# A hybrid decoder step on one core: weight splits in half-size pieces through two rooms, gate scratch in a tile of its own, and later stores of the compression weights

## The chip, the cores and the metric

The kernel runs on one core of a Trainium2 chip. The time is the device time of one execution in microseconds (us); the kernel before was run three times. All sizes are fixed: 1024 prompt tokens, 8 sample tokens with 2048 cached tokens each, model width 1024.

## What is computed

One layer of a decoder with two parallel head groups, cut to what matters here:

```python
h = rms_norm(x, norm_g); proj = h @ w_in
b_gate, c_gate, conv_in, z_conv, q, kv, gate_logits, z_attn = split(proj)
# group 1: short convolution over the tokens
conv = b_gate * short_conv(c_gate * conv_in) * silu(z_conv)
# group 2: sparse attention, three branches per query block of 128 tokens
kv_cmp = compress_blocks(kv[cmp], cmp_pe, cmp_w)        # 32 tokens -> 1 row
o = g0 * attend(q, kv_cmp) + g1 * attend(q, top blocks) + g2 * attend(q, last 512 tokens)
attn = o * silu(z_attn)
y = x + concat(conv, attn) @ w_out                       # 1024 x 1024
```

The prompt goes through this with its own keys and values, the 8 samples with gathered cache rows. Outputs are y, the new key/value rows and the conv state.

## The kernel before, in words

All large products are in float32 split into two parts: a high part, which ScalarE (ACT) makes as a rounding copy (`copy`, line 75), and a low part, the difference, which VectorE (DVE) or GpSimd (POOL) subtracts (`sub`, line 79). A product is three matmuls of such parts (lines 227 to 229 for the channel products, `chan_mm`).

The program has two long stages that run as merged streams (`merge`, line 30: generators give costs, and the stream that is least far along is recorded next) and then a last one. The tile framework orders the instructions of each engine from this and from the tiles' readers and writers; each engine runs its list in order, and so does the queue that SyncE (SP) feeds.

1. `phase0` (line 534): norm, key/value and query projections. In its second loop over 9 token tiles, `cw_fetch` and `cw_split` bring in the compression weights `cw` and split them; for t = 5 to 8 line 595 stores a quarter of them (`cw_d`, a DRAM scratch), and after the loop line 607 multiplies with them. From here to 236 us the rest of the projections follow.
2. The attention of the prompt, `attn_stream` (line 762): 32 units, 8 query blocks `qi` of 128 tokens x 2 groups x 2 head pairs. A unit does, for branch 1 (selected and compressed, tiles `P1a` and `P0`) and branch 2 (window, tile `P2`): `scores` (matmuls `s`, line 804, then `softmax`, the row maximum and mask on DVE, line 792, and the exponent on ACT, line 794), `scale` (reciprocal on DVE, 844; gate and denominator on POOL, 849 and 853), then transposes (`pt`, 878), their split into `ph` and `pl`, and the products `o` (888). `double` (770) and `prep` (776, then `q`) make the next unit's queries; `finish` (903) multiplies into `mixA`. Beside it runs `conv_stream`: channel products `mm` from weights `wraw` that SP loads (line 173) and ACT and POOL split into `wh` and `wl`; `conv_use` (line 707) consumes them. A z product ends in `silu2` (line 699): tanh on ACT from the bank (line 700, `mixC<-mm`), then a product on DVE (line 701).
3. Samples, output projection: `prefetch` loads `wo_d` and `cw_d` back through the POOL queue, and so on to the end at 937.5 us.

Two side jobs ride on the first units of stage 2, and they are what the change touches.

- `w_split` (line 908): the first 512 columns of `w_out`, 8 row chunks. Even unit 2k loads chunk k (256 KB, line 914) into the low half of a tile `P1b`; odd unit 2k+1 splits it (ACT copy of 512 columns, POOL subtraction of 512 columns) and stores both halves to `wo_d[k]` (512 KB, line 918). The tile has one room: the load of chunk k+1 overwrites what the store of chunk k reads. From query block 4 on, the attention itself uses the tile `P1b`.
- `z_attn` (line 703): the silu of z for the attention's own gate, one piece of 128 tokens (4 channels x 128 = 512 columns) for each query block. Its tanh goes into the scratch tile `acc` (one room), which `conv_use` (line 719) also uses for the convolution.

```python
if ui % 2 == 0:
    wsp = at.tile([128, 2, 512], F32R, name="P1b")
    SP.dma_start(f(wsp[:, 1]), w_out[:, ui // 2, 0:512])
else:
    copy(ACT, wsp[:, 0], f(wsp[:, 1]))
    sub(POOL, wsp[:, 1], f(wsp[:, 1]), f(wsp[:, 0]))
    SP.dma_start(wo_d[ui // 2], f(wsp))
```

Of the kernel before, what the change touches and what calls it, by code (L numbers as in the profile page):

```python
# [60 lines left out]
def hymba_step_kernel(ctx, tc, io):  # L61
# [8 lines left out]
    def f(ap):  # L70
        return ap.bitcast(F32)
# [6 lines left out]
    def sub(eng, out, a, b):  # L78
        return eng.tensor_tensor(out, a, b, OP.subtract)  # L79
# [455 lines left out]
    def phase0():  # L535
        nonlocal qkv
        x_load(0)
        SP.dma_start(gbc, bcast_rows(io["norm_g"], D))
        SP.dma_start(idt, io["c_ident"])
        c0 = wl0(COL_KV, 256)  # L540
        c0[1](0)
        c0[1](1)
        x_load(1)
        c0[1](2, xsp)
        c0[1](3, xsp)
        x_load(2)
        SP.dma_start(rope0, io["c_rope"])
        turns = [x_norm(0)]
        turns.pop(0)()
        tab0 = rope_tables(io["k_gain"][0, 0], 0, 1.0)  # L550
        for i in range(4):
            c0[2](i, *E0)
        x_load(3)
        turns.append(x_norm(1))
        turns.pop(0)()
        c1 = wl0(COL_KV + 256, 256)
        for t in range(NT):
            if t + 4 < NT:
                x_load(t + 4)
            if t + 2 < NT:  # L560
                turns.append(x_norm(t + 2))
            o = tok_mm(t, c0[0], 256)
            if turns:
                turns.pop(0)()
            posted(1)
            rows, _ = kv_rows(wk, o, t, 0, *tab0)
            if t < 8:
                posts.append((lambda kd=twice(wk, rows, 4), t=t: cmp_transposes(kd, t), 1))
            if t == 7:
                tab1 = rope_tables(io["k_gain"][0, 1], 1, 1.0)  # L570
            if t in (1, 2):
                for i in (2 * t - 2, 2 * t - 1):
                    c1[2](i)
            if t < 2:
                for i in (2 * t, 2 * t + 1):
                    c1[1](i)
            yield 3900
        posted(9)
        xss.close()
        cw = xcp2.enter_context(pool("cw")).tile([128, 16, 2, 128], F32R, name="cw")  # L580
        c2 = wl0(COL_KV + 512, 280)
        for t in range(NT):
            kv_tile(t, c1[0], 256, 1, tab1)
            if t == SM:
                small_things()
            if t == 0:
                c2[1](0)
                c2[1](1)
            if t in (2, 4):
                c2[2](t // 2 - 1)  # L590
                c2[1](t // 2 + 1)
            if 0 < t < 5:
                cw_split()
            if t > 4:
                SP.dma_start(cw_d[t - 5], f(cw[:, t * 4 - 20:t * 4 - 16]))
            if t < 4:
                cw_split = cw_fetch(wk, cw, t)
            yield 3400

        posted(9)  # L600

        kc = wk.tile([128, 2, 2, 33], F32, name="kc")
        for j in range(2):
            o = bank("cc")
            for rho in range(16):
                for X in (XH, XL):
                    PE.matmul(o[:, :66], cw[:, rho, j], X[:, 2 * j:2 * j + 2, rho::16],
                              start=rho == 0 and X is XH, stop=rho == 15 and X is XL)
            ov = o[:, :66].rearrange("p (g c) -> p g c", g=2)
            copy(ACT, kc[0:64, j], ov[64:128])  # L610
            copy(ACT, kc[64:128, j], ov[0:64])
            DVE.tensor_tensor(kc[:, j], ov, kc[:, j], OP.add)
            copy(DVE, pew[:, j:j + 1], kc[:, j, 0, 32:33])
            DVE.tensor_scalar(kc[:, j, :, :32], kc[:, j, :, :32], pew[:, j:j + 1], None, op0=OP.add)
        copy(ACT, kpc, kc[:, 0, :, :32])
        sub(DVE, kpc[64:128], kc[64:128, 0, :, :32], f(kpc[64:128]))
        p = bank("tp")
        for g in range(2):
            PE.transpose(p[:32, g * 64:g * 64 + 64], kc[0:64, 1, g, :32], ident[:64, :64])
        pv = p[:32, :128].rearrange("p (g d) -> p g d", g=2)  # L620
        copy(ACT, vpc[:32, :, 0:64], pv)
        sub(DVE, vpc[:32, :, 64:128], pv, f(vpc[:32, :, 0:64]))
        yield 8000
        xcp2.close()
        xcs.close()

        qkv = left.enter_context(pool("qkv"))
        K[2] = qkv.tile([128, 2, SEQ], F32R, name="k2")
        V[2] = qkv.tile([128, 8, 2, 128], F32R, name="v2")
        qt.extend(qkv.tile([128, 512], F32, name=f"q{t}") for t in range(8))  # L630

        c2[2](2)
        c2[2](3)
        tab2 = rope_tables(io["k_gain"][0, 2], 0, 1.0)
        nxt = wl0(COL_Q, 256)
        for t in range(NT):
            kv_tile(t, c2[0], 280, 2, tab2)
            if t == 0:
                nxt[1](0)
                nxt[1](1)  # L640
            if t in (2, 4):
                nxt[2](t // 2 - 1)
                nxt[1](t // 2 + 1)
            yield 3600
        posted(9)
        tabq = rope_tables(io["q_gain"][0], 1, 0.125)
        for which in range(2):
            nxt[2](2)
            nxt[2](3)
            w = nxt[0]  # L650
            nxt = wl0(COL_Q + 256, 256)
            for t in (8, *range(8)):
                q_tile(t, w, which, tabq)
                if which == 0:
                    if t == 0:
                        nxt[1](0)
                        nxt[1](1)
                    if t in (2, 4):
                        nxt[2](t // 2 - 1)
                        nxt[1](t // 2 + 1)  # L660
                yield 2700
# [30 lines left out]
    cvs = ExitStack()  # L692
    cv = cvs.enter_context(pool("conv", "right"))
    cu = cv.tile([128, 2 + NTOK], F32, name="cu")
    uo = cv.tile([128, 4, 16], F32, name="uo")
    POOL.memset(cu[:, 0:2], 0.0)

# [3 lines left out]
        DVE.scalar_tensor_tensor(m, t, 1.0, z, op0=OP.add, op1=OP.mult)  # L701

    def z_attn(a, n):
        t = cv.tile([128, 512], F32, name="acc")[:, :4 * n].rearrange("p (a c) -> p a c", a=4)
        silu2(mixA[:, :, a:a + n], mixA[:, :, a:a + n], t)

    def conv_use(kind, i, c, o, s):
# [7 lines left out]
        else:  # L715
            DVE.tensor_tensor(u, o, u, OP.mult)
            n = CH if c < 2 else SEQ - 2 * CH
            w, b = cvw[:, i, :], cvw[:, i, 3:4]
            acc = cv.tile([128, 512], F32, name="acc")
            a, lo = acc[:, :n], c * CH  # L720
            ACT.activation(a, cu[:, lo:lo + n], AF.Copy, scale=w[:, 0:1])
            for r in (1, 2):
# [12 lines left out]
    def conv_stream():  # L735
        yield from chan
        p = bank("mm")
        for i in range(4):
            PE.transpose(p[:10, i * 128:(i + 1) * 128], uo[:, i, :10], ident)
        ur = cv.tile([128, 512], F32, name="acc")[:10]  # L740
        copy(ACT, ur, p[:10])
        SP.dma_start(io["p_conv"].rearrange("l b r c -> (l b r) c"), ur[0:2])
        SP.dma_start(io["s_conv"].rearrange("l b r c -> (l b) r c")[:, 1, :], ur[2:10])
        yield 400

    at = left.enter_context(pool("attn"))
# [15 lines left out]
    def attn_stream():  # L762
# [141 lines left out]
            if g == 1 and hp == 1:  # L904
                done[qi] = True

        wsp = None

        def w_split(ui):

            nonlocal wsp
            if ui % 2 == 0:
                wsp = at.tile([128, 2, 512], F32R, name="P1b")
                SP.dma_start(f(wsp[:, 1]), w_out[:, ui // 2, 0:512])
            else:
                copy(ACT, wsp[:, 0], f(wsp[:, 1]))
                sub(POOL, wsp[:, 1], f(wsp[:, 1]), f(wsp[:, 0]))
                SP.dma_start(wo_d[ui // 2], f(wsp))

        qq = prep(double(units[0]))  # L920
        masks()
        pend = []
        for ui, u in enumerate(units):
            o = [None]
            share = PACE[u[0]]
            if ui % 4 == 2 and u[0] < 7:
                z_attn(u[0] * 128 + 128, 128)
            elif ui == 3:
                z_attn(SEQ, 8)
            a = at.tile([128, 1024], F32, name="P1a")  # L930
            P1 = (a[:, 0:512], a[:, 512:1024]) if u[0] < 4 else (a, at.tile([128, 1024], F32, name="P1b"))
            P2 = at.tile([128, 2, 640], F32, name="P2")
            P2 = (P2[:, 0], P2[:, 1])
            if u[0] < 4:
                w_split(ui)
            stt = at.tile([128, 3, 6], F32, name="stat", bufs=2)
            more = ui + 1 < len(units)
            qd = nxt = None
            for br, P in ((1, P1), (2, P2)):

                held = []
                for k in range(max(2, len(pend) + LAG)):
# [4 lines left out]
                        cost += scores(u, qq, br, k, P, stt)  # L947
                    if k == 1:
                        scale(u, br, P, stt)
                    if 0 <= k - LAG < len(pend):  # L950
                        tr, mm, c = pend[k - LAG]
                        held.append((mm, tr() if tr else None))
                        cost += c
                        if len(held) > DEPTH:
                            mm, h = held.pop(0)
                            mm(h)
# [5 lines left out]
                    mm(h)  # L962
                    yield 0
                pend = av_items(u, br, P, o)
                if ui == 0 and br == 1:
                    z_attn(0, 128)
            pend.append((None, lambda h, u=u, o=o: finish(u, o), 0))
            qq = nxt
        held = None
# [595 lines left out]
```

## Time and profile before

| | us |
|---|---|
| three runs | 938.84, 940.31, 941.01 (median 940.31) |
| profiled execution, its own time | 939.31 |
| its span on the core | 937.5 |
| around the span | 1.8 |
| PE / DVE / ACT / POOL busy | 878.3 / 613.4 / 549.5 / 419.0 |
| mean granted TensorE clock | 0.967 |

PE is TensorE's matmuls, DVE VectorE, ACT ScalarE, POOL GpSimd, SP the engine that issues most DMAs. A granted clock of 1.00 is TensorE's full 2.4 GHz, 0.50 is 1.2 GHz. "L79" is line 79. In timelines, the bracket at the end of a row is the engine's idle time just before the instruction and who ended it.

### The profile page before, as it was taken

To read this page: it belongs to the slowest core of one execution; us is meant where nothing else is said; L and a number is where in the kernel's file an instruction comes from. 1 tells how busy PE (TensorE), PEld (TensorE's weight loads), DVE (VectorE), ACT (ScalarE), POOL (GpSimd) and SP (SyncE) were. 2 spreads that over 40 slices of the span, in tenths; PEclk is the share of its full clock that TensorE was granted. 3 is DMA by queue.
4 is the path that set the end of the run, shared out by engine and by line. 5 is a ranking of instruction groups with operands and counts; after the bars stand their busy time and mean duration, and the time that the engine had idled before them with its cause. 6 is when DMAs were issued, how large, how long until landed. Compare 5 with 4: busy or idle time off the path is not lost.

```text
span 937.5 us, 16984 instructions
## 1 busy us (share of the span) xinstructions
PE 878.3 (94%) x5789; PEld 788.5 (84%) x5789; DVE 613.4 (65%) x1702; ACT 549.5 (59%) x1489; POOL 419.0 (45%) x570
## 2 busy tenths in 40 slices
PE   7988899999899999999999999999989999799897
PEld 6988899899779889899988988999868887577674
DVE  5896735597745455775685577567736546867885
ACT  5764533633567556565665656566646767566671
POOL 4232331412266544543435343543655553368762
PEclk7999969999899999999999999999999999799999
DMA  7513531311133201000100001000786653747640
GB/s 245 155 57 96 167 97 46 102 57 31 45 114 113 90 24 24 12 13 22 35 24 23 23 1 35 24 1 1 238 285 232 236 171 124 270 133 253 223 133 25
DMA packets 57059, 93.78 MB, mean 100 GB/s; under 512 B 10502, under 2 KB 39118, under 8 KB 54796
## 3 DMA queue, kind: packets, MB, share of 16 engines
q1 hardware_dynamic: 48332, 52.84, 18.0%
q0 software_dynamic: 8640, 39.85, 12.9%
q8 instruction: 46, 0.75, 0.3%
q14 instruction: 41, 0.34, 0.1%
HBM read 79.49 MB, written 17.39 MB: 103 GB/s over the span
## 4 chain that ended last, share of the span: by engine, by line
PE 45%; DVE 8%; ACT 7%; POOL 4%; issue 3%; DMA 2%; ACTq 0%; POOLq 0%; DVEq 0%
PE o L888 7%; PE pt L878 5%; PE s L804 5%; PE mm L229 5%; PE mm L228 4%; PE mm L227 4%; PE mm L1399 1%; PE mm L1397 1%; PE pt L1025 1%; PE mm L1046 1%; PE mm L1398 1%; ACT ph L75 1%; PE om L1399 1%; PE om L1398 1%; PE om L1397 1%
## 5 line engine op out<-in xcount | busy, mean ns | idle before, releaser
L227 PE MATMUL mm<-hH,wh 128*128 128x384 f32 (+1 forms) x480 | 158.5, 330 | 0.0
L229 PE MATMUL mm<-hH,wl 128*128 128x384 f32 (+1 forms) x480 | 156.3, 326 | 0.0
L228 PE MATMUL mm<-hL,wh 128*128 128x384 f32 (+1 forms) x480 | 155.9, 325 | 0.0
L79 POOL TENSOR_TENSOR wl<-wraw,wh 128x256 fp32r<-128x256 f32 (+1 forms) x120 | 89.6, 763 | 114.2 <-ACT wh L75 82.6
L79 DVE TENSOR_TENSOR pl<-pt,ph 128x512 fp32r<-128x512 f32 (+1 forms) x164 | 102.6, 636 | 50.9 <-ACT ph L75 49.9
L75 ACT ACTIVATE ph<-pt 128x512 fp32r<-128x512 f32 (+1 forms) x164 | 88.3, 549 | 71.0 <-PE pt L878 70.1
L804 PE MATMUL s<-k,q 128*128 128x320 f32 (+8 forms) x416 | 96.6, 335 | 4.1 <-ACT q L75 1.5
L212 PE MATMUL mm<-wh,hH 128*128 128x256 f32 (+1 forms) x320 | 94.6, 296 | 0.5 <-ACT hH L75 0.5
L213 PE MATMUL mm<-wl,hH 128*128 128x256 f32 (+1 forms) x320 | 94.2, 294 | 0.0
L214 PE MATMUL mm<-wh,hL 128*128 128x256 f32 (+1 forms) x320 | 94.0, 294 | 0.0
L227 PEld LDWEIGHTS mm<-hH,wh 128*128 128x128 f32 x480 | 92.3, 192 | 0.6 <-DVE mixC L701 0.5
L228 PEld LDWEIGHTS mm<-hL,wh 128*128 128x128 f32 x480 | 92.5, 193 | 0.3 <-issue 0.2
L229 PEld LDWEIGHTS mm<-hH,wl 128*128 128x128 f32 x480 | 92.4, 192 | 0.1
L888 PE MATMUL o<-ph,v 128*128 128x256 f32 x264 | 74.8, 302 | 3.7 <-ACT ph L75 3.3
L888 PE MATMUL o<-pl,v 128*128 128x256 f32 x264 | 73.4, 300 | 1.7 <-DVE pl L79 1.5
L804 PEld LDWEIGHTS s<-k,q 128*128 128x128 f32 x416 | 67.4, 192 | 8.4 <-ACT q L75 2.0
L794 ACT ACTIVATE P<-P,stat 128x32 f32<-128x32 f32 (+5 forms) x128 | 63.9, 499 | 3.7 <-DVE stat L792 3.0
L212 PEld LDWEIGHTS mm<-wh,hH 128*128 128x128 f32 x320 | 63.7, 199 | 1.0 <-ACT hH L75 1.0
L214 PEld LDWEIGHTS mm<-wh,hL 128*128 128x128 f32 x320 | 63.7, 199 | 0.2 <-DVE hL L79 0.2
L213 PEld LDWEIGHTS mm<-wl,hH 128*128 128x128 f32 x320 | 63.8, 200 | 0.0
L849 POOL TENSOR_SCALAR P<-P,stat,gates 128x32 f32<-128x32 f32 x64 | 22.7, 367 | 89.0 <-DVE stat L844 77.3
L853 POOL TENSOR_SCALAR P<-P,stat,gates 128x640 f32<-128x640 f32 (+4 forms) x64 | 47.5, 752 | 29.4 <-DVE stat L844 28.8
(365 smaller groups left out, 2372.3 us busy)
## 6 DMA issues: line engine op xcount, KB each, us to landing
wraw<-in_w_in_dram SPq DMA_DIRECT2D x56, 256.0 KB
xt<-in_x_prompt_dram SPq DMA_DIRECT2D x8, 512.0 KB
wo_d<-P1b SPq DMA_DIRECT2D x8, 512.0 KB
wo<-wo_d POOLq DMA_DIRECT2D x8, 512.0 KB, 4.5
sd<-in_state_win_kv_dram SPq DMA_DIRECT2D x8, 512.0 KB
out_s_win_dram<-in_state_win_kv_dram SPq DMA_DIRECT2D x8, 511.0 KB
xr<-in_x_prompt_dram SPq DMA_DIRECT2D x14, 256.0 KB
out_y_prompt_dram<-xr SPq DMA_DIRECT2D x14, 256.0 KB
```

Source lines behind the costliest of these rows:

```text
L75: return ACT.activation(out, in_, AF.Copy)
L79: return eng.tensor_tensor(out, a, b, OP.subtract)
L212: PE.matmul(o[:, :n], hH[t // 3][:, k, s], wh, start=k == 0, stop=False)
L213: PE.matmul(o[:, :n], hH[t // 3][:, k, s], wl, start=False, stop=False)
L214: PE.matmul(o[:, :n], hL[t // 3][:, k, s], wh, start=False, stop=k == 7)
L227: PE.matmul(o[:, :n], wh, hH[c][:, k], start=k == 0, stop=False)
L228: PE.matmul(o[:, :n], wh, hL[c][:, k], start=False, stop=False)
L229: PE.matmul(o[:, :n], wl, hH[c][:, k], start=False, stop=k == 7)
L794: return lambda: ACT.activation(P, P, AF.Exp, bias=stt[:, 0, c:c + 1], scale=-1.0, accum_out=stt[:, 1, c:c + 1])
L804: PE.matmul(s[:, a:b], q[:, i], k, start=first, stop=not first)
L853: POOL.tensor_scalar(P[i][:, :n], P[i][:, :n], stt[:, 2, c + i:c + i + 1], gates[:, qi, gt:gt + 1], op0=OP.mult, op1=OP.mult)
L888: PE.matmul(o[0][:, :256], v, X[:, y * 256:y * 256 + 256], start=br == 1 and x == 0 and y == 0 and X is h[0], stop=last and y + 1 == len(p ...
```

## The change

Three edits:

1. The four stores of `cw_d` stand behind the products that read `cw` (line 622) instead of in the loop.
2. The tanh of `z_attn` gets a tile `zt` of 256 columns; each query block's piece is cut into two of 64 tokens, given out at two units instead of one. The scratch `acc` shrinks to 384 columns, and the conv state at the end goes out in two halves (four DMAs instead of two).
3. `w_split` works in 16 pieces of 256 columns. The tile is made once and has two rooms; piece x uses room x % 2. `w_fetch(x + 1)` (128 KB) stands at the start of unit x; the split of piece x stands behind `scale` of the window branch of unit x, and its store is 256 KB in runs of 1 KB.

```diff
@@ phase0
-            if t > 4:
-                SP.dma_start(cw_d[t - 5], f(cw[:, t * 4 - 20:t * 4 - 16]))
...
+        for i in range(4):
+            SP.dma_start(cw_d[i], f(cw[:, i * 4:i * 4 + 4]))
         yield 8000
@@ conv scratch
+    zt = cv.tile([128, 256], F32, name="zt")
...
     def z_attn(a, n):
-        t = cv.tile([128, 512], F32, name="acc")[:, :4 * n].rearrange("p (a c) -> p a c", a=4)
+        t = zt[:, :4 * n].rearrange("p (a c) -> p a c", a=4)
...
-            acc = cv.tile([128, 512], F32, name="acc")
+            acc = cv.tile([128, CH], F32, name="acc")
@@ attn_stream
+        wsp = at.tile([128, 2, 2, 256], F32R, name="P1b")
+
+        def w_fetch(x):
+            k, a = divmod(x, 2)
+            SP.dma_start(f(wsp[:, x % 2, 1]), w_out[:, k, a * 256:a * 256 + 256])
+
+        def w_split(x):
+            k, a = divmod(x, 2)
+            h, l = wsp[:, x % 2, 0], wsp[:, x % 2, 1]
+            copy(ACT, h, f(l))
+            sub(POOL, l, f(l), f(h))
+            SP.dma_start(wo_d[k][:, :, a * 256:a * 256 + 256], f(wsp[:, x % 2]))
...
+        w_fetch(0)
...
-            if ui % 4 == 2 and u[0] < 7:
-                z_attn(u[0] * 128 + 128, 128)
-            elif ui == 3:
+            if ui % 4 > 1 and u[0] < 7:
+                z_attn(u[0] * 128 + ui % 2 * 64 + 128, 64)
+            elif ui == 1:
                 z_attn(SEQ, 8)
...
-            if u[0] < 4:
-                w_split(ui)
+            if ui < 15:
+                w_fetch(ui + 1)
...
                     if k == 1:
                         scale(u, br, P, stt)
+                    if k == 1 and br == 2 and ui < 16:
+                        w_split(ui)
...
-                if ui == 0 and br == 1:
-                    z_attn(0, 128)
+                if ui == 0:
+                    z_attn(br * 64 - 64, 64)
```

How the instructions stand, at three places. The first is SP's queue around the fifth to seventh chunk; `P1b<-in_w_out_dram` is a load of `w_out`, `wo_d<-P1b` a store, `wraw` a load of conv weights. Before:

```order
L914 DMA P1b<-in_w_out_dram 128x512
L173 DMA wraw<-in_w_in_dram 128x4x128 x2
L918 DMA wo_d_83<-P1b 128x1024
L914 DMA P1b<-in_w_out_dram 128x512
L918 DMA wo_d_84<-P1b 128x1024
```

and now:

```order
L915 DMA P1b<-in_w_out_dram 128x256 x2
L173 DMA wraw<-in_w_in_dram 128x4x128
L922 DMA wo_d_83<-P1b 256x1x256
L173 DMA wraw<-in_w_in_dram 128x4x128
L922 DMA wo_d_84<-P1b 256x1x256
L915 DMA P1b<-in_w_out_dram 128x256 x2
L922 DMA wo_d_84<-P1b 256x1x256
```

The store of wo_d_83 in this piece is that of piece 9, the two of wo_d_84 are those of pieces 10 and 11; the loads that stand behind the store of piece 10 are those of pieces 11 and 12. A conv weight load now stands between the stores of pieces 9 and 10.

The second place is POOL's list in the same stretch (`wl` is a conv weight split, `P1a` the scale of branch 1, `qd` the next queries, `mixA` the end of a unit). Before:

```order
L849 TENSOR_SCALAR P_3470<-P_3470,stat,gates 128x32 x2
L853 TENSOR_SCALAR P1a<-P1a,stat,gates 128x256 x2
L79 TENSOR_TENSOR wl<-wraw,wh 128x256 x2
L770 COPY qd<-q_1859 128x256
L903 TENSOR_TENSOR mixA<-ot,mixA 128x128
L79 TENSOR_TENSOR P1b<-P1b 128x512
```

and now:

```order
L852 TENSOR_SCALAR P_3471<-P_3471,stat,gates 128x32 x2
L856 TENSOR_SCALAR P1a<-P1a,stat,gates 128x256 x2
L79 TENSOR_TENSOR wl<-wraw,wh 128x256
L79 TENSOR_TENSOR P1b<-P1b 128x256 x2
L79 TENSOR_TENSOR wl<-wraw,wh 128x256
L773 COPY qd<-q_1859 128x256
L906 TENSOR_TENSOR mixA<-ot,mixA 128x128
```

Two pieces (9 and 10) are subtracted between the two conv weight splits, where one whole chunk stood behind `mixA`.

The third place is ACT's list right after; `mixC<-mm` is the tanh of a conv z product, `P1a,stat` and `P` are exponents. Before:

```order
L794 ACTIVATE P_3954,stat<-P_3954,stat 128x256
L75 ACTIVATE ph<-pt 128x512
L75 ACTIVATE P1b<-P1b 128x512
L75 ACTIVATE ph<-pt 128x256
L794 ACTIVATE P_3954,stat<-P_3954,stat 128x256
L700 ACTIVATE mixC<-mm 128x384
L794 ACTIVATE P1a,stat<-P1a,stat 128x256
```

and now:

```order
L797 ACTIVATE P_3964,stat<-P_3964,stat 128x256
L75 ACTIVATE ph<-pt 128x512
L797 ACTIVATE P_3964,stat<-P_3964,stat 128x256
L75 ACTIVATE ph<-pt 128x256
L75 ACTIVATE P1b<-P1b 128x256
L701 ACTIVATE mixC<-mm 128x384
L75 ACTIVATE P1b<-P1b 128x256
L797 ACTIVATE P1a,stat<-P1a,stat 128x256
```

The copies of pieces 11 and 12 now stand right before and right behind the tanh `mixC<-mm`, ahead of the exponents of `P1a`. The tanh into `zt` (16 pieces and a small one for the samples) all stand ahead of this place; of the nine into `acc` (8 and the small one), five stand ahead of it and four later.

In the first stage the order of every engine is the same before and now: the four stores of `cw_d` stand at the same place in SP's queue, behind the same rows.

## Rows read from the trace of the kernel before

**Rows 1.** The page, busy time of the engines over the span (share, number of instructions); the first row, PE.

```profile
PE 878.3 (94%) x5789; PEld 788.5 (84%) x5789; DVE 613.4 (65%) x1702; ACT 549.5 (59%) x1489; POOL 419.0 (45%) x570
```

**Rows 2.** Windows over the first part and over the middle of the attention; columns: stretch, its length, busy us (instructions) of PE, PE weight load, DVE, ACT, POOL, the granted TensorE clock, DMA share, GB/s.

```profile
240.00:320.00 80.00, 72.11 (x441) 65.29 (x440) 43.52 (x187) 51.03 (x173) 45.47 (x82) 0.94 0.29 96
320.00:680.00 360.00, 350.00 (x2366) 321.14 (x2365) 238.24 (x636) 224.30 (x589) 167.39 (x255) 1.00 0.12 34
```

**Rows 3.** Windows of a few microseconds, same columns: the half clock after the attention's start, and a wait with what follows it.

```profile
244.70:251.50 6.80, 6.38 (x22) 5.51 (x23) 4.03 (x25) 4.26 (x17) 2.76 (x5) 0.50 0.01 2
...
313.00:316.40 3.40, 1.70 (x11) 1.38 (x10) 1.29 (x3) 2.72 (x13) 2.85 (x5) 0.99 0.38 154
316.40:319.80 3.40, 3.40 (x15) 3.40 (x14) 1.32 (x5) 0.91 (x3) 0.51 (x2) 0.50 0.00 0
```

**Rows 4.** Timeline of PE: start, duration, instruction, and in brackets the idle time before it and who ended it.

```profile
243.34 0.46 PE L804 MATMUL s<-k,q 128*128 128x160 f32 x2 [1.51 <-ACT q L75]
245.12 0.71 PE L804 MATMUL s<-k,q 128*128 128x160 f32 x2 [1.33 <-DVE q L79]
...
314.89 0.39 PE L888 MATMUL o<-ph,v 128*128 128x256 f32 x1 [1.71 <-ACT ph L75]
...
398.71 0.38 PE L888 MATMUL o<-pl,v 128*128 128x256 f32 x1 [0.86 <-DVE pl L79]
```

**Rows 5.** The chain of waits around 310 us, followed back from its end: start, duration, what.

```profile
305.41 1.27 POOL P1b L79
...
306.69 2.65 DMA wo_d<-P1b
...
309.36 2.67 DMA P1b<-in_w_out_dram
...
312.14 0.63 ACT P1b L75
...
314.36 0.49 ACT ph L75
...
314.89 0.39 PE o L888
```

**Rows 6.** The list of waits from 236 to 330 us: who waited <- for what: us in total, times, longest.

```profile
ACT P1b L75 <- DMA P1b<-in_w_out_dram: 6.1, 3, 3.1
```

**Rows 7.** Timeline of SP's DMA issues (the duration is that of the issue, not of the transfer).

```profile
262.95 0.33 SPq L918 DMA_DIRECT2D wo_d<-P1b  x1
264.33 0.38 SPq L173 DMA_DIRECT2D wraw<-in_w_in_dram  x1
266.26 0.33 SPq L914 DMA_DIRECT2D P1b<-in_w_out_dram  x1
...
273.93 0.33 SPq L914 DMA_DIRECT2D P1b<-in_w_out_dram  x1
...
297.11 0.33 SPq L918 DMA_DIRECT2D wo_d<-P1b  x1
299.73 0.33 SPq L914 DMA_DIRECT2D P1b<-in_w_out_dram  x1
```

**Rows 8.** Timeline of ACT: at the attention's start, at a split, and at the third place of the order above.

```profile
242.38 0.63 ACT L700 ACTIVATE acc<-mixA 128x512 f32<-128x512 f32 x1
242.92 0.36 ACT L75 ACTIVATE q<-pt 128x256 fp32r<-128x256 f32 x1
...
276.67 0.63 ACT L75 ACTIVATE P1b<-P1b 128x512 fp32r<-128x512 f32 x1 [1.65 <-DMA P1b<-in_w_out_dram]
...
289.49 0.49 ACT L700 ACTIVATE mixC<-mm 128x384 f32<-128x384 f32 x1 [2.39 <-PE mm L229]
290.94 0.51 ACT L794 ACTIVATE P1a<-P1a,stat 128x256 f32<-128x256 f32 x1 [0.96 <-DVE stat L792]
```

**Rows 9.** Timeline of POOL at the second place of the order above.

```profile
283.34 1.09 POOL L853 TENSOR_SCALAR P1a<-P1a,stat,gates 128x256 f32<-128x256 f32 x2
284.39 1.44 POOL L79 TENSOR_TENSOR wl<-wraw,wh 128x256 fp32r<-128x256 f32 x2
...
286.54 1.29 POOL L79 TENSOR_TENSOR P1b<-P1b 128x512 fp32r<-128x512 f32 x1
```

**Rows 10.** Timeline of DVE there: the product behind the tanh, and the first softmax behind it.

```profile
290.01 0.56 DVE L701 SCALAR_TENSOR_TENSOR mixC<-mixC,mm 128x384 f32<-128x384 f32 x1 [2.71 <-ACT mixC L700]
290.48 0.42 DVE L792 CUSTOM_DVE_ANT_0 P1a<-s,mask 128x256 f32<-128x256 f32 x1
```

**Rows 11.** Timeline of PE there: the scores of branch 1 and those of branch 2, which write the next buffers of `s` (there are two).

```profile
290.00 0.56 PE L804 MATMUL s<-k,q 128*128 128x288 f32 x3
...
291.17 0.47 PE L804 MATMUL s<-k,q 128*128 128x256 f32 x2
```

**Rows 12.** Groups by line and shape from 236 to 580 us: shape and count, then busy us, mean ns of one, idle time before.

```profile
L700 ACT ACTIVATE acc<-mixA 128x512 f32<-128x512 f32 x8 | 5.0, 627 | 6.7 <-DVE mixC L725 5.1 <-DVE mixA L701 1.6
L75 ACT ACTIVATE P1b<-P1b 128x512 fp32r<-128x512 f32 x8 | 5.0, 625 | 6.1 <-DMA P1b<-in_w_out_dram 6.1
L75 ACT ACTIVATE wh<-wraw 128x256 fp32r<-128x256 f32 x52 | 20.8, 410 | 3.0 <-PE mm L228 2.4
L79 POOL TENSOR_TENSOR wl<-wraw,wh 128x256 fp32r<-128x256 f32 x52 | 38.0, 744 | 26.7 <-ACT wh L75 19.7 <-PE mm L229 6.2 <-ACT P L794 0.7
L79 POOL TENSOR_TENSOR P1b<-P1b 128x512 fp32r<-128x512 f32 x8 | 10.3, 1286 | 4.7 <-ACT P1b L75 4.7
```

**Rows 13.** The instructions on the tile `cw_d`: count, duration of the issue (min/median/max ns), first and last start.

```profile
L595 SPq DMA_DIRECT2D cw_d<-cw x4: 333/431/601, 97.4 to 121.8; - x4
```

More of the change, by code (lines that the diff above doesn't have):

```diff
@@ L739, in conv_stream @@
             PE.transpose(p[:10, i * 128:(i + 1) * 128], uo[:, i, :10], ident)
[L740 to L743, printed above, removed]
+        for a in range(2):
+            c = slice(a * 256, a * 256 + 256)
+            ur = cv.tile([128, CH], F32, name="acc")[:10, :256] if a else zt[:10]
+            copy(ACT, ur, p[:10, c])
+            SP.dma_start(io["p_conv"].rearrange("l b r c -> (l b r) c")[:, c], ur[0:2])
+            SP.dma_start(io["s_conv"].rearrange("l b r c -> (l b) r c")[:, 1, c], ur[2:10])
         yield 400
@@ L905, in finish @@
                 done[qi] = True
[L907 to L918, printed above, removed]
+        wsp = at.tile([128, 2, 2, 256], F32R, name="P1b")
[8 more added lines that the diff above has]
+            SP.dma_start(wo_d[k][:, :, a * 256:a * 256 + 256], f(wsp[:, x % 2]))
         qq = prep(double(units[0]))
         masks()
+        w_fetch(0)
         pend = []
```

## The prediction

> **What bounds the kernel now.** I read the page's busy times first: PE works for 94% of the span [rows 1]. So only a stretch in which PE stands idle, or runs at the half clock, has anything to give. The windows show where: from 320 to 680 us PE is busy for 350.00 of 360 us at a clock of 1.00; from 240 to 320 us, the units that carry the weight splits and most gate pieces, it is busy for 72.11 of 80 us and its clock is 0.94 [rows 2]. The change acts in that stretch. PE's timeline shows its idle places: 1.51 and 1.33 us at the start, 1.71 us before 314.89 [rows 4]. The reader is to see that the last one costs twice: the small windows show PE busy for 1.70 of 3.40 us and then 3.40 us at a clock of 0.50 [rows 3], which is work of 1.70 us at full clock stretched to 3.40.
>
> The chain of waits says where the 1.71 us comes from [rows 5]: POOL ends the low half of one chunk, its store takes 2.65 us, only then may the next load start (one room), 2.67 us, and ACT, in order, stands before the copy; the exponents and `ph` are behind it. The list of waits has this at 3.1 us, the longest of three [rows 6].
>
> **The change part by part.** A measurement of this kernel tells about 0.2% (1.9 us) from no change.
>
> (a) The stores of `cw_d`: the four issues [rows 13] stand in the same place of SP's queue, behind the same rows, before and now, and so does all else up to 236 us. Their data is read back only at the end of the attention. Cost 0, bound 0 on both sides, because no engine's order differs there.
>
> (b) The gate pieces: each 512-column tanh of 627 ns becomes two of 256 columns, for which the nearest row is the 256-column copy at 410 ns [rows 12]. At the start, ACT's first tanh stands before the copy of `q` for which PE waits [rows 8, 4]: 0.627 - 0.410 = 0.2 us earlier, -0.2. In all, ACT gets 8 x (2 x 410 - 627) = +1.5 us and, for the split, 8 x (2 x 410 - 625) = +1.6 us; POOL gets 8 x (2 x 744 - 1286) = +1.6 us. In 240 to 320 us ACT is busy for 51.03 and POOL for 45.47 of 80 us [rows 2], so most of it hides; if the cover were gone it would be the 1.5 us of the tanh. Bounds 0 to +1.5, and I take +0.3, near the lower end, since the engines have over 28 us free there. That later tanh no longer share `acc` with the convolution gives nothing: PE's idle 0.86 us in that part waits for DVE's `pl` [rows 4].
>
> (c) The old wait. With two rooms, a piece's load need not wait for the store of the piece just before. The stores of whole chunks begin at 297.11 and 306.69 [rows 7, 5], so two units last 9.6 us; a room's cycle of copy, subtraction, store and load is 0.4 + 0.7 + 2.6 + 2.7 = 6.4 us [rows 12, 7, 5]. So the wait at 312 us goes: -1.71 of idle, and -1.7 of half clock behind it [rows 3].
>
> (d) A new wait. The rooms have slack only if pieces come evenly, and the order does not have them so: POOL now does pieces 9 and 10 back to back. In the times of before: POOL's scale of `P1a` ends at 283.34 + 1.09 = 284.43 [rows 9]; then a `wl` of 0.72 and piece 9 of 0.72 to 0.74 [rows 9, 12], so its store can go at 285.87; piece 10 to 286.6 and the second `wl` to 287.3. SP has a conv weight load between the two stores, which waits for that `wl`; so the store of piece 10 leaves at 287.7 and the load of piece 11 (the room of piece 9) right behind it. That room's store lands 2.62 us after 285.87, at 288.5 (297.11 to 299.73 [rows 7]), or after 3.31, at 289.2, as the store at 262.95 did beside a weight load (262.95 to 266.26 [rows 7]). The load of 256 KB took 2.67 and 276.67 - 273.93 = 2.74 us [rows 5, 7, 8], and 512 KB out took no longer, so size sets little; a half-size load is bounded by 1.3 (half) and 2.74, and I take 2.7, the row that it is nearest to. So piece 11 lands at 291.2 (289.8 to 291.9), and its copy of 0.41 ends at 291.6.
>
> Behind that copy on ACT stands the tanh `mixC`, which began at 289.49 [rows 8]: 2.1 us late (0.7 to 2.8). Behind the tanh, in order on DVE, stand `mixC` at 290.01 and the softmax of `P1a` at 290.48 [rows 10], and PE's next scores at 291.17 need the bank which that softmax reads [rows 11]: it ends at 290.90, a slack of 0.3. So PE stands for 2.1 - 0.3 = +1.8 us (0.4 to 2.5). What is late next are the exponents of `P1a` (290.94 [rows 8]), which stand behind the copy of piece 12.
>
> The Trainium skill speaks against smaller pieces: "DMA: Bandwidth & Descriptors", section Bandwidth, asks for transfers of 1 MiB and more, and its section on the anatomy of one DMA puts some 2 us of fixed cost beside the bytes (measured there on another path than SP's). By that (an estimate from the page: 2.6 us for the store, 2.3 for the load) piece 11 would land at 290.8, and the sum be 0.4 us lower; the rows agree that size hardly counts.
>
> (e) The half clock behind the new wait. After 1.71 us of idle the clock fell for 3.40 us [rows 3, 4]; after 0.86 us at 398 us it did not, since 320 to 680 us has 1.00 throughout [rows 4, 2]. 1.8 is nearer to the first: +1.7 (0 to +1.7).
>
> Sum: -0.2 + 0.3 - 1.71 - 1.7 + 1.8 + 1.7 = +0.2 us, on the profiled execution's own 939.31, so 939.5. That execution lies 1.0 below the median of the three runs (938.84 to 941.01), and I do not know on which side of the middle the next one falls; half of this goes on top: **940.0**.
>
> **The rivals.**
>
> First, the new wait comes, but the clock stays at 2.4 GHz: -1.7, so **938.3**. For it: only one idle place of such a length is followed by a fall here with certainty. Against it: 1.51 and 1.33 us at 243 to 245 us are followed by 6.80 us at 0.50 too [rows 4, 3]. The Trainium skill's "TensorE: Matmul & The Clock Gate", Part 1, says that the monitor of activity runs free of the kernel's start; so the same idle time may be followed by a fall in one place and not in another, which the pair of rows 4 and 3 can neither show nor exclude.
>
> Second, the load of piece 11 lands before the tanh is due (a half-size load at 1.3 us and DVE slack), and nothing replaces the old wait: -1.8 - 1.7, so **936.5**. For it: a half-size transfer is in no row. Against it: by the earliest bound it still lands at 289.8, after 289.49.
>
> Third, slower: piece 12 decides. Its room's store is that of piece 10, at 287.7, and two loads and a store share the queue then. With 3.31 us for the store it lands at 291.0, with 2.74 for the load at 293.7; the copy ends at 294.1, and the exponents of `P1a`, 290.94 before [rows 8], are 3.2 us late where the scores were 2.1 late: +1.1 of idle. The idle then spreads over two places and the half clock lasts for twice as long, as the 6.80 us at 0.50 after the two idle places at the start [rows 3, 4]: +1.7. So 939.5 + 2.8 + 0.5 = **942.8**. It decides from the point at which piece 12 lands after about 293 us. For it: the 3.31 us beside a weight load, and the runs of 1 KB instead of 4 KB in the store. Against it: in the values that I took, 2.62 and 2.7, it lands at 293.0 at the latest, and DVE and POOL keep work.
>
> That the change does not do what it says holds for its first part alone (a), and is in all cases.
>
> **How the numbers follow.** Chances: forecast 0.40, first rival 0.24, second 0.16, third 0.20. With 0.2% either side of the median of before, faster means under 938.43 and slower over 942.19. Faster: all of the second (0.16) and some half of the first, which lies at the bound (0.11): 0.27. Slower: the third, save a little (0.18). Same: 0.55. The range runs from the second to the third, 936.5 to 942.8, and leaves out about half of each of these two, 0.18. The forecast's own range, by the bounds of (b), (d) and (e), is 938.3 to 941.9.
>
> **What would show it.** Right: the copy of a `P1b` piece in the list of waits near 288 to 292 us, behind a load, with the tanh `mixC` and PE's scores late by about 2 us, then a window at 0.50; no wait of ACT for a load near 312 us, and 313 to 320 us busy at a clock of 1.00. Wrong: PE without idle there (second rival); idle with a clock of 1.00 behind it (first); two idle places there, and some 7 us at 0.50 (third); or a difference in the first 236 us, which part (a) excludes.

## The result

The change made the kernel slower: 947.23 us (median of 4 runs, 946.09 to 947.97) against 940.37 (4 runs, 938.84 to 941.01), a ratio of 1.0080 with a 95% interval of 1.0060 to 1.0101. The forecast was 940.0 with a range up to 942.8. Executions with a mean granted clock of 0.83 (one of e3, 970.78 us, and one of the kernel before, 968.61 us) are left out of all medians and ratios below.

### The profile after

The profiled execution has a span of 946.2 us, 8.7 more than before; it is the slowest of the four runs, and the medians differ by 6.9. Windows of the kernel after, columns as in [rows 2]: stretch, length, busy us of PE, PE weight load, DVE, ACT, POOL, granted clock, DMA share, GB/s.

```profile
120.00:236.00 116.00, 114.02 (x843) 112.96 (x843) 71.56 (x266) 48.71 (x173) 27.65 (x39) 0.94 0.22 66
...
240.00:320.00 80.00, 69.34 (x408) 63.33 (x407) 48.69 (x189) 52.65 (x185) 45.04 (x85) 0.89 0.33 100
320.00:680.00 360.00, 351.12 (x2363) 323.21 (x2362) 236.26 (x636) 222.62 (x591) 165.03 (x254) 1.00 0.11 32
```

From 240 to 320 us PE is busy for 69.34 us at a clock of 0.89 where it was 72.11 at 0.94 [rows 2]: the loss is in the stage of the change. ACT and POOL have much the same work as before there, and DVE is busy for 5.2 us more, 3.0 of them in one held instruction that is shown below; so PE loses by waits, not by work. The small windows, same columns, show three places:

```profile
263.00:267.80 4.80, 1.75 (x13) 1.25 (x11) 4.74 (x14) 2.19 (x10) 2.82 (x5) 1.00 0.76 210
267.80:271.30 3.50, 3.50 (x14) 3.01 (x14) 2.38 (x10) 2.75 (x12) 2.65 (x7) 0.51 0.30 88
295.00:298.50 3.50, 0.89 (x8) 0.78 (x7) 1.60 (x10) 2.17 (x8) 1.49 (x3) 1.00 0.24 71
298.50:302.00 3.50, 3.50 (x15) 3.50 (x14) 2.20 (x8) 2.46 (x10) 2.81 (x7) 0.51 0.51 164
313.00:316.40 3.40, 3.40 (x22) 3.37 (x21) 1.03 (x3) 0.70 (x3) 2.81 (x6) 1.00 0.51 152
316.40:319.80 3.40, 3.37 (x26) 3.15 (x25) 2.38 (x12) 2.13 (x9) 0.40 (x1) 1.00 0.02 8
```

The last two are the old place of [rows 3], where PE now works at the full clock. The middle two are the wait that was forecast near 291 us. The first two were not forecast: PE idle, then the half clock, near 265 us. PE's timeline of the kernel after:

```profile
266.51 0.41 PE L807 MATMUL s<-k,q 128*128 128x128 f32 x2 [3.05 <-DVE stat L795]
...
276.27 0.41 PE L807 MATMUL s<-k,q 128*128 128x128 f32 x2 [0.70 <-DVE stat L795]
...
297.75 0.47 PE L807 MATMUL s<-k,q 128*128 128x256 f32 x2 [2.61 <-DVE stat L795]
```

**The place that was forecast.** SP's issues, then ACT, kernel after:

```profile
289.98 0.53 SPq L922 DMA_DIRECT2D wo_d<-P1b  x1
291.38 0.38 SPq L173 DMA_DIRECT2D wraw<-in_w_in_dram  x1
291.81 0.53 SPq L922 DMA_DIRECT2D wo_d<-P1b  x1
292.42 2.83 SPq L915 DMA_DIRECT2D P1b<-in_w_out_dram  x2
...
295.77 0.42 ACT L75 ACTIVATE P1b<-P1b 128x256 fp32r<-128x256 f32 x1 [5.04 <-DMA P1b<-in_w_out_dram]
296.09 0.47 ACT L701 ACTIVATE mixC<-mm 128x384 f32<-128x384 f32 x1
297.13 0.42 ACT L75 ACTIVATE P1b<-P1b 128x256 fp32r<-128x256 f32 x1 [0.57 <-POOL P1b L79]
```

The store of piece 9 leaves at 289.98, the load of piece 11 at 292.42, and its copy begins at 295.77: 3.35 us for a load of 128 KB, beside a store and a weight load, more than the 2.7 taken from [rows 5, 7]. The copy stands for 5.04 us, the tanh and the softmax behind it.

**The place that was not.** DVE, POOL and ACT of the kernel after, near 265 us:

```profile
262.28 3.42 DVE L702 SCALAR_TENSOR_TENSOR mixA<-zt,mixA 128x256 f32<-128x256 f32 x1 [0.55 <-ACT zt L701]
265.62 0.42 DVE L702 SCALAR_TENSOR_TENSOR mixC<-mixC,mm 128x264 f32<-128x264 f32 x1
```

```profile
261.94 0.74 POOL L79 TENSOR_TENSOR wl<-wraw,wh 128x256 fp32r<-128x256 f32 x1
262.63 0.74 POOL L79 TENSOR_TENSOR P1b<-P1b 128x256 fp32r<-128x256 f32 x1
263.33 1.41 POOL L79 TENSOR_TENSOR wl<-wraw,wh 128x256 fp32r<-128x256 f32 x2
264.69 0.72 POOL L79 TENSOR_TENSOR P1b<-P1b 128x256 fp32r<-128x256 f32 x1
267.29 0.40 POOL L773 COPY qd<-q 128x256 f32<-128x256 f32 x1 [1.88 <-PE pt L779]
```

```profile
261.85 0.40 ACT L701 ACTIVATE zt<-mixA 128x256 f32<-128x256 f32 x1
...
265.73 0.42 ACT L701 ACTIVATE zt<-mixA 128x256 f32<-128x256 f32 x1 [2.48 <-DVE mixA L702]
266.28 0.40 ACT L797 ACTIVATE P1a<-P1a,stat 128x128 f32<-128x128 f32 x1
```

The reader is to see a product of z that takes 3.42 us where the same instruction takes 0.42 elsewhere. It began when its tanh was done, and ended at 265.70, 0.29 us behind the last of POOL's subtractions (265.41), which follow one another without a gap. The next softmax on DVE, and the next tanh and exponent on ACT, stand behind it, and PE for 3.05 us.

### The profile page after: what moved, and what is told of

Read it like the earlier page. It is cut to its first block, busy times and chain, and to the rows that moved or that the text cites. A ratio compares the mean times of both kernels' runs of the same rounds, so it can differ in the third digit from the quotient of the medians.

```text
span 946.2 us, 17054 instructions
## 1 busy us (share of the span) xinstructions
PE 883.3 (93%) x5789; PEld 793.2 (84%) x5789; DVE 619.8 (66%) x1710; ACT 552.2 (58%) x1506; POOL 420.1 (44%) x578
## 4 chain that ended last, share of the span: by engine, by line
PE 53%; DVE 11%; ACT 7%; issue 4%; POOL 4%; DMA 1%; ACTq 0%; POOLq 0%; DVEq 0%; SPq 0%
PE o L891 7%; PE mm L229 6%; PE pt L881 6%; PE s L807 6%; PE mm L227 6%; PE mm L228 6%; PE mm L1406 1%; PE mm L1404 1%; PE pt L1032 1%; PE mm L1053 1%; PE mm L1405 1%; ACT ph L75 1%; PE mm L213 1%; PE mm L214 1%; PE mm L212 1%
```

## The experiments

Each time stands against runs of the kernel before on the same chip; the medians of before lay between 939.12 and 939.81 in these groups, single runs between 934.0 and 944.5. The places named are those of one profiled execution; its time can lie 3 us beside the median (e2: 946.14 and 942.73).

**e2: the second edit alone** (`zt` and the halves), weight chunks as before.

> Only the second edit (tanh of z in a tile of its own, pieces of 64 tokens); stores of cw_d and the weight splits as before. Theory A (a DVE product of two SBUF operands, mixA<-zt,mixA, cannot run while POOL works without a gap): the product near 262 us meets POOL's gapless run (257.4 to 264.6 us before) and takes 2 to 3 us instead of 0.42; PE stands 2 to 3 us behind it and the clock may fall, so 943 to 945.5 us. Theory B (the loss belongs to the weight pieces, whose wait was forecast near 291 us): 939.5 to 941.5, no product over 1 us. The wait for the load at 312 us stays under both.

Measured: 942.73 us, ratio 1.0030 (1.0005 to 1.0054). The time lies between the two ranges, just under theory A's. Its cause does not hold at its place: no product was held near 262. PE stood elsewhere. ACT, then DVE, then PE, of e2:

```profile
270.15 0.40 ACT L701 ACTIVATE zt<-mixA 128x256 f32<-128x256 f32 x1
271.93 0.42 ACT L701 ACTIVATE zt<-mixA 128x256 f32<-128x256 f32 x1 [1.38 <-DVE mixA L702]
272.84 0.42 ACT L701 ACTIVATE zt<-mixA 128x256 f32<-128x256 f32 x1 [0.49 <-DVE mixA L702]
273.16 0.47 ACT L701 ACTIVATE mixC<-mm 128x384 f32<-128x384 f32 x1
```

```profile
270.58 1.31 DVE L702 SCALAR_TENSOR_TENSOR mixA<-zt,mixA 128x256 f32<-128x256 f32 x1 [1.25 <-ACT zt L701]
```

```profile
275.08 0.41 PE L807 MATMUL s<-k,q 128*128 128x128 f32 x2 [2.56 <-DVE stat L795]
...
299.08 0.39 PE L891 MATMUL o<-ph,v 128*128 128x256 f32 x1 [1.57 <-ACT ph L75]
```

Freed from `acc`, the pieces of all query blocks come early, and with one room tanh and product take turns, 0.9 us a piece. Three of them stand ahead of the conv's tanh, and the softmax behind that. One of the products was held after all, for 1.31 us instead of 0.42, until 0.27 us behind POOL's subtraction of a whole chunk (270.33 to 271.62). The last line of the expectation fell too: no copy waits for a load at 312 us any more; one does at 296 us (2.33 us), with 1.57 us of idle on PE before 299.08.

**e3: the third edit alone** (16 pieces, two rooms), z in `acc` as before.

> Only the third edit (weight split in 16 pieces through two rooms); z's tanh in acc as before. Theory A: no stretched DVE product, the copy of a piece still waits about 5 us for its load near 295 us, PE stands about 2.5 us there with a half clock behind it, and the wait at 312 us is gone: 940 to 942.5 us. Theory B: the whole loss is here, 945 to 948 us.

Measured: 941.49 us, ratio 1.0026 (1.0000 to 1.0052), as theory A has it. PE stands before 295.49, nowhere else for over 0.5 between 250 and 330:

```profile
295.49 0.47 PE L804 MATMUL s<-k,q 128*128 128x256 f32 x2 [2.54 <-DVE stat L792]
```

The copy of piece 11 had waited for 4.93 us for its load. In this execution the clock did not fall behind the 2.54 us (1.00 in 295 to 302 us), which it did behind 2.61 us in the kernel after.

**e4: the position of the split alone.**

```diff
-            if u[0] < 4:
+            if u[0] < 4 and ui % 2 == 0:
                 w_split(ui)
...
                         scale(u, br, P, stt)
+                    if k == 1 and br == 2 and u[0] < 4 and ui % 2:
+                        w_split(ui)
```

> The kernel before with one thing of the change alone: whole chunks through one room, but the split stands behind scale of the window branch of the odd unit instead of at its start. Theory A: the load has one more half unit, so ACT waits under 1 us for it and PE's 1.71 us at 314.89 with the half clock behind it go: 936.5 to 938.5 us. Rival: the later split makes the next load later by as much, the wait only moves: 939.5 to 942 us.

Measured: 940.01 us, ratio 0.9992 (0.9969 to 1.0016). My expectation fell. The copy of the last chunk begins at 312.15 us behind the same wait of 3.10, since the engines' lists came out almost the same: where the split is written hardly decides where it runs.

**e6, e7, e11, e13: the hold by itself.** Four kernels with a measurement behind the last result of the kernel before.

> The kernel before with a measurement appended behind its last result (the outputs are those of before): DVE product of two SBUF operands, 128x256, started about 0.4 us after POOL began n subtractions of 128x256 without a gap. Theory A: DVE's instruction lasts until POOL's run is over, 0.43 us for n = 0, about 0.8 for n = 1, 1.5 for 2, 3 for 4, 6 for 8; with an operand in PSUM 0.4 to 0.5 beside n = 4; with gaps in POOL's run it ends at the first gap. Rival (the two engines share the access by turns): it grows by a factor of up to two and no more, 0.4 to 0.9 us for any n. The rows with POOL's one-operand scaling and DVE's one-operand product tell which forms are concerned; no theory fixes these beforehand.

> As e6_port, but POOL's subtractions write four places in turn, so that none waits for the one before it, as in the kernel's own splits (0.72 us each, the next one starts 0.04 us before the last one ends). Theory A2: the DVE product of two SBUF operands gets in only where POOL's instructions leave a gap; in e6_port each waited for the one before it (0.80 us apart), which left one. Then it lasts about 0.7 us beside n = 1, 1.3 beside 2, 2.7 beside 4, 5.5 beside 8, and 0.42 with an operand in PSUM. Rival: it gets in at the next boundary, 0.4 to 0.8 us for any n, and the 3.42 us at 262 us in the changed kernel has another cause.

> Again the kernel before with a measurement behind it: one DVE product of two SBUF operands beside five POOL subtractions of 128x256 (0.7 us each). Varied: POOL's output F32 or fp32r (as the kernel's splits have it), DVE arriving early, in the second or in a later subtraction, DVE's pattern flat or 4 rows of 64 (as z's halves), DVE's product or its subtraction to fp32r. Theory A3: with one of these forms DVE is not let in between POOL's instructions and lasts until the run is over (up to 3.5 us); that form is the one at 262 us in the changed kernel. Rival: 0.4 to 1.1 us in all cases, let in at the next boundary as in the two measurements before, and what holds it for 3.42 us at 262 us stays open.

> The last measurement of this kind, behind the kernel before: six POOL subtractions to fp32r in a row, each with an input that ACT made just before (so each has a wait of its own, long met), in another place or in place as the weight pieces have it, with three one-operand scalings ahead or not; one DVE product of two SBUF operands, flat or 4 rows of 64, arrives in the middle of the run. If such a run holds DVE to its end, as at 262 us in the changed kernel: 1.5 to 3.5 us in the cases concerned, ending about 0.3 us behind POOL's last. Rival: 0.4 to 1.0 us in all of them, and why that one was held for 3.42 us stays open.

In all four the rival held: never more than 0.98 us. With POOL's run of eight subtractions in e6 (6.40 us) the product took 0.60, beside e7's eight without a pause (5.67 us) 0.60 too, in the middle of e13's run 0.58 (DVE, then POOL, of e6):

```profile
942.29 0.60 DVE L1516 SCALAR_TENSOR_TENSOR mixC<-mixC 128x256 f32<-128x256 f32 x1 [3.21 <-ACT mixC L75]
```

```profile
941.89 6.40 POOL L1525 TENSOR_TENSOR mixA<-mixA 128x256 f32<-128x256 f32 x8 [0.62 <-ACT mixA L1531]
```

With an operand in PSUM it took 0.42, which is no wait. So in these runs DVE waits for the POOL instruction that is under way and gets in at the next boundary. This does not give 3.42 us.

**e8: z's halves in `acc`**, the rest as in the change.

> The changed kernel, but the tanh of z's halves goes into acc, so that the convolution's use of that tile holds back the pieces of the later query blocks (8 of 16 stay early); weight pieces as in the change. If the early pieces of the later query blocks cost (ACT and DVE in turn through one room, ahead of the tanh and softmax of the conv and the scores), 943 to 945; if all of it is the two or three places near 262 and 295 us, which stay, 946 to 948.

Measured: 944.01 us, ratio 1.0049 (1.0025 to 1.0073). PE still stands for 3.07 us at 266 and 2.46 at 297; the 0.70 near 276 is 0.47, as it was at 272 before. The held product is there again, in a tile that is not `zt`:

```profile
262.04 3.43 DVE L701 SCALAR_TENSOR_TENSOR mixA<-acc,mixA 128x256 f32<-128x256 f32 x1 [0.53 <-ACT acc L700]
```

For the hold it is the early place in the lists, not the tile, that matters. The time lies in the first range, but these places do not say why: from the attention's start to 344 us the same matmuls lose 4.4 us against the kernel before, in the kernel after 4.7.

**e9, e10: a third room** for the weight pieces from piece 5 on, without and with the second edit.

```diff
+        rooms = [wsp[:, 0], wsp[:, 1]]
+        def room(x):
+            return rooms[x % 2 if x < 5 else x % 3]
...
+            if x == 5:
+                rooms.append(qkv.tile([128, 2, 256], F32R, name="q0"))
```

> e3_wsplit_only with a third room for the weight pieces from piece 5 on (the tile of the first query block's queries, done by then). If the waits of PE are those of copies for a load, behind a store, then neither the one near 295 nor the old one at 312 us is there: 936 to 938 us. If POOL's late subtractions set it, the wait stays: 940 to 942.

> The changed kernel with the third room. The wait near 295 us goes with its half clock (2.6 + 1.7 us): 942 to 944.5 us, with the stretched DVE product near 262 us still there or not, by where POOL's run falls. If that wait is not worth what its place says, 946 to 948.

Measured: e9 943.10 us, ratio 1.0045 (1.0026 to 1.0063); e10 946.35, ratio 1.0069 (1.0046 to 1.0092). By their medians both expectations fell. In e9 the copy of piece 12, one piece further on, stands for 5.12 us until 294.94, before the same tanh: three pieces are now subtracted close together, and the list has one more copy ahead of the tanh. PE stands for 2.42 us there, with a half clock behind it (0.50 from 296.7 to 300.1 us). In e10 the corresponding wait of the copy is 4.01 us; PE stands for only 1.30 us there, and the clock stays at 1.00. That place did shrink, and the profiled execution (944.04 us) is in the expected range; the median is not, and why stays open. In e9 the room was not what was short; the order of the list puts a copy ahead of the tanh that its load cannot serve. e10 adds a row on the hold:

```profile
262.30 3.80 DVE L702 SCALAR_TENSOR_TENSOR mixA<-zt,mixA 128x256 f32<-128x256 f32 x1 [0.84 <-ACT zt L701]
```

POOL's run has one subtraction more there, ends at 265.82, and the product at 266.10.

**e12: the old wait alone taken away.** The last chunk gets rooms of its own and is loaded at unit 10.

```diff
+            if ui == 10:
+                last.extend(qkv.tile([128, 512], F32R, name=n) for n in ("q0", "q1"))
+                SP.dma_start(f(last[1]), w_out[:, 7, 0:512])
+            if ui == 15:
+                h, l = last
+                copy(ACT, h, f(l))
+                sub(POOL, l, f(l), f(h))
+                SP.dma_start(wo_d[7][:, 0], f(h))
+                SP.dma_start(wo_d[7][:, 1], f(l))
+            elif ui % 2 == 0 and ui < 14:
...
+            elif ui < 14:
...
```

> The kernel before with the old wait alone taken away: whole chunks through one room, but the last chunk has rooms of its own (the tiles of the first two query blocks' queries) and is loaded at unit 10, so that its copy stands before no store. If the wait at 312 us costs what its rows say (1.71 us of idle and 1.7 of half clock): 936 to 938 us, PE without idle at 315 us. If a following engine takes its place: 939 to 941.

Measured: 936.58 us, ratio 0.9963 (0.9949 to 0.9977), faster than both kernels. Its windows, columns as above, at the old place of [rows 3]:

```profile
313.00:316.40 3.40, 3.40 (x23) 3.40 (x22) 1.68 (x7) 2.30 (x10) 1.79 (x4) 1.00 0.02 5
316.40:319.80 3.40, 3.40 (x25) 3.09 (x24) 2.35 (x9) 1.99 (x6) 0.77 (x2) 1.00 0.01 2
```

0.37% of 940 is 3.5 us (2.2 to 4.8), where the prediction had 3.4.

**e14: the hold, in the kernel after.** Pieces 3 and 4 subtracted on DVE, so that POOL's run is shorter.

```diff
-            sub(POOL, l, f(l), f(h))
+            sub(DVE if x in (3, 4) else POOL, l, f(l), f(h))
```

> The changed kernel with the subtractions of weight pieces 3 and 4 on DVE instead of POOL: POOL's gapless run near 262 us loses these two and ends about 1.4 us earlier. If POOL's run holds DVE there: the first DVE instruction with two SBUF operands in the run (now the subtraction of piece 3, before z's product) ends about 0.3 us behind the run's new end, 1.5 to 2.2 us instead of 0.42, z's product behind it takes 0.42; PE stands 1.5 to 2 us there instead of 3.06: 944.5 to 946.5 us. If the hold belongs to z's product itself, it stays at 3.4 us: 947 or more. If the hold is not there at all, PE stands under 1 us there: 942 to 944.5.

Measured: 942.42 us, ratio 1.0035 (1.0017 to 1.0053); faster than expected: by the time alone, the case without a hold (942 to 944.5). The place shows the hold, as theory A has it. DVE, then POOL, of e14:

```profile
261.39 2.67 DVE L79 TENSOR_TENSOR P1b<-P1b 128x256 fp32r<-128x256 f32 x1
263.98 0.41 DVE L702 SCALAR_TENSOR_TENSOR mixA<-zt,mixA 128x256 f32<-128x256 f32 x1
```

```profile
261.66 2.11 POOL L79 TENSOR_TENSOR wl<-wraw,wh 128x256 fp32r<-128x256 f32 x3
```

Now another instruction is held, the first with two SBUF operands that meets the run. The run ends at 263.77, the held one at 264.06, and z's product behind it takes 0.41. Both sizes are above the expected ones (2.67 against 1.5 to 2.2, and 2.23 us of idle on PE, instead of 3.05, against 1.5 to 2). So it is POOL's run that holds DVE, not z's product: in four kernels with four ends of the run (265.41, 265.20, 265.82, 263.77) the held instruction ended 0.27 to 0.29 us behind it. The 4.8 us between the medians of the kernel after and of e14 are mostly not from this place: the same two matmuls of `o` stand 18.96 us apart before (261.56 and 280.52), 22.33 in the kernel after and 21.43 in e14, so 0.9 us.

## Why the prediction was wrong

- **(a) The stores of `cw_d`: right.** 114.02 us of PE's work in 120 to 236 us against 114.01 before. No run has this edit alone.
- **(b) The gate pieces: the step that failed.** It read "the engines have over 28 us free there" and took +0.3 with a bound of +1.5. The free time is an average over 80 us; the pieces stand in lists that run in order, and each delays what is behind it. In the kernel after, all 17 tanh of z run between 242.0 and 280.1 us; before, they were spread from 242.4 to 572.4. Measured: +2.8 us (0.5 to 5.1) for the second edit alone (e2), by a turn-taking of ACT and DVE through one room that the prediction did not look at, and a wait for a load that came elsewhere. Together with the third edit it also gave the hold near 262 us, which neither edit has alone: 3.05 us of idle and the half clock behind it, 3.2 us in the table below. With 3.2 in place of +0.3 the sum would be 942.9, just beyond the range's end of 942.8. The remark that the later pieces' freedom from `acc` "gives nothing" had the sign wrong: it costs, since they come early.
- **(c) The old wait: right**, in place and size (e12).
- **(d) The new wait: right in its place and chain, too small in size.** PE stands for 2.61 us in the kernel after and 2.54 in e3, against 1.8 and a bound of 2.5; the load took 3.35 us, not 2.7.
- **(e) The half clock: right** for the kernel after (0.51 in 298.5 to 302 us). The first rival's mechanism is real too: in e3 the clock stayed at 1.00 behind 2.54 us of idle, while it fell behind 2.46 in e8 and 2.42 in e9 and e14. So the length of the idle time alone does not decide it here. The forecast's own range leaves the bound of 0 of (e) out at its lower end: with it, it begins at 936.6, not at 938.3.
- **The start of the attention** was taken as -0.2. PE's two waits there are 0.3 us shorter, but the clock stayed low for longer. Kernel after, then e14, where the same two waits (1.30 and 1.28 us) stand ahead; before it was 6.80 us [rows 3]:

```profile
243.90:254.10 10.20, 9.59 (x33) 8.74 (x34) 6.20 (x30) 6.36 (x25) 3.86 (x8) 0.50 0.23 73
```

```profile
245.40:248.80 3.40, 3.40 (x13) 3.31 (x13) 2.07 (x15) 1.97 (x10) 0.72 (x1) 0.50 0.00 0
```

- **The sum of the places.** The table follows the same matmuls through both traces (start in us).

| matmul | before | after | later by | what lies between |
|---|---|---|---|---|
| `pt<-ident,qd` | 240.22 | 239.86 | -0.4 | |
| `o<-pl,vpc` | 261.56 | 262.29 | 0.7 | the start: +1.1 |
| `o<-pl,vpc` | 270.36 | 274.31 | 3.9 | the hold and its half clock: +3.2 |
| `o<-pl,vpc` | 289.41 | 293.31 | 3.9 | |
| `o<-pl,vpc` | 308.40 | 316.62 | 8.2 | the new wait and its half clock: +4.3 |
| `o<-pl,vpc` | 321.46 | 326.09 | 4.6 | the old wait, gone: -3.6 |
| `mm<-hH,wh` | 343.98 | 348.34 | 4.4 | -0.3 |

The stage of the change thus loses 4.7 us of the 8.7, where the prediction's sum had 0.2: 2.9 more for the hold than (b) had, 0.8 more for (d) and (e) and 1.3 more at the start, less 0.5 in the last two rows. The low stretch at the start lasts 10.2 us in e8 and e10 too, but 3.4 in e2 and e14, behind much the same waits; whether it follows from the change stays open.
- **The rest of the 8.7 us** came where the program is the same. At 486.2 us the clock falls for 3.4 us (0.51; before, 1.00 there), and near 690 and 920 us. Windows of before, then of after:

```profile
680.00:700.00 20.00, 16.47 (x83) 12.87 (x84) 6.41 (x11) 8.54 (x18) 10.96 (x16) 0.91 0.86 303
915.00:937.50 22.50, 16.60 (x80) 10.95 (x78) 11.71 (x26) 3.22 (x11) 3.86 (x4) 1.00 0.08 25
```

```profile
684.00:704.00 20.00, 16.51 (x81) 13.09 (x80) 6.23 (x11) 7.23 (x15) 9.79 (x14) 0.83 0.84 288
922.00:946.20 24.20, 17.92 (x79) 12.26 (x77) 11.49 (x25) 3.23 (x11) 3.65 (x4) 0.88 0.07 24
```

The clock fell for longer at the start of the last stage, and once in the tail. The fall in the tail also comes without the change, in e4, whose lists are almost those of before:

```profile
915.00:937.50 22.50, 18.87 (x83) 12.96 (x81) 12.37 (x27) 3.75 (x12) 4.53 (x4) 0.92 0.06 24
```

Still, the medians differ by 6.9 us, 2.2 more than the stage of the change explains, and the granted clock of the four runs after is 0.959 to 0.962, where runs of before have 0.961 to 0.976. So some of this lasts over runs; whether it follows from the change was not tried.
- **The third rival** gave a time nearer to the result by a mechanism that did not come: piece 12's copy waited 0.57 us, for POOL and not for its load.

## What to carry to other kernels

Free time of an engine over a stage hides nothing by itself: look in each engine's list for what stands behind the moved instruction, and who waits for that. In this case the lists that show the early pieces were at hand before the run. Work that loses its reason to wait (a scratch of its own) moves to the front of the list, and may be worse there. Where one wait is to go, take away what makes that one wait, as e12 does; smaller pieces moved it (e3), and a third room moved it by one piece (e9).

## What was not expected of the hardware

A DVE instruction with two operands in SBUF can be held for as long as POOL runs without a gap: 0.42 us became 3.42, 3.43, 3.80 and, in e14, 2.67. The trace of the kernel before had shown a small case, in which 0.69 us became 2.74 (DVE, then POOL):

```profile
828.85 2.74 DVE L79 TENSOR_TENSOR vhl<-sd,vhl 128x512 fp32r<-128x512 f32 x1 [1.05 <-ACT vhl L75]
```

```profile
828.51 1.29 POOL L79 TENSOR_TENSOR vhl<-sd,vhl 128x512 fp32r<-128x512 f32 x1
829.74 1.29 POOL L79 TENSOR_TENSOR ml<-mixC,mh 128x512 fp32r<-128x512 f32 x1
```

The same trace also has the other case, in the kernel's own work and with the other engines busy: POOL does four subtractions without a gap, and a DVE instruction with two SBUF operands is let in behind the first of them (65.55); it takes 0.72 us instead of 0.28 (DVE, then POOL):

```profile
64.98 0.72 DVE L279 TENSOR_TENSOR rows<-ra,rb 128x128 f32<-128x128 f32 x1
```

```profile
64.80 3.04 POOL L79 TENSOR_TENSOR wl<-wraw,wh 128x256 fp32r<-128x256 f32 x4 [1.72 <-PE mm L217]
```

The Trainium skill ("SBUF — State Buffer", section Who interferes with whom) states that a DVE instruction with two SBUF inputs contends with a GpSimd instruction that reads SBUF; its section SBUF: two separate sides adds that the one that starts first has the access for its whole instruction. The four measurements by themselves agree (up to 0.98 us, let in at a boundary; 0.42 with a PSUM operand), and so does the row at 64.98 us; the hold over several of POOL's instructions goes beyond it. What lets DVE in at a boundary in the one case and not in the other stays open: POOL's output type, waits, in-place form and the arrival in the run were varied in e7, e11 and e13, and none brought the hold about.
